# Inverse roots of the norms per head: root function of ScalarE and reciprocal, or Newton steps on VectorE

## The chip, the core and the metric

The kernel runs on one core of a Trainium2 chip. The metric is the device time in microseconds (us) of one execution. The median of 3 runs of the kernel before is 2390.03 us (2385.15 to 2393.97). The engines are TensorE (PE; its weight loads are listed as PEld), VectorE (DVE), ScalarE (ACT), GpSimd (POOL) and SyncE (SP, which issues the DMAs).

## The reference

One step of a two-layer backbone over 384 tokens (128 of context, 256 latent) of width 1024, in fp32. Each layer is a gated FFN, a mixer and a second gated FFN, each with a residual and a layer norm. The mixer projects its input once and feeds three branches: window attention, neighbourhood attention and a recurrence (RWKV-7) of 8 heads of 64 channels in two directions. Two places in the recurrence's branch normalise per head:

```python
kk = split_heads((k * lp['k_k']).astype(f32), C_HEADS)
kk = kk / jnp.maximum(jnp.sqrt(jnp.sum(kk * kk, axis=-1, keepdims=True)), 1e-12)
...
mu = y.mean(-1, keepdims=True)
var = jnp.mean(jnp.square(y - mu), -1, keepdims=True)
yn = ((y - mu) * lax.rsqrt(var + GN_EPS)).reshape(B, L, C_WIDTH) * lp['gn_g'] + lp['gn_b']
```

## The kernel before, in words

Activations lie with the channels on the partitions and the 384 tokens along the free axis. All big products are made from weights and activations split into a high and a low part (three matmuls for each block of 128 x 128). The weights stream in units of 8 blocks: a DMA brings `raw`, ACT copies it to `hi`, DVE subtracts to get `lo` (`fetch`, called by `Stream.take`).

A layer runs FFN 1, the mixer, FFN 2. The mixer has three stages. In `attention` the eight head pairs of the two attentions (`heads_pair`: scores, a softmax on DVE and ACT, transposes and products with the values) run beside `front_fill`, a generator of projections and gates; the first pieces of the recurrence's projections (`conv_gen` with the names tw, al, k0, r0, v0, k1, r1, v1) are among them. In the second stage `rwkv_gen` works through four pairs of heads p = 0 to 3. For each pair, `rwkv_prepare` makes decays and keys, `rwkv_chunks` solves small triangular systems for chunks of 64 tokens (DVE steps that depend on each other, small matmuls, copies out of PSUM), and `rwkv_scan` carries the state over the chunks, normalises the output per head, and multiplies by the gate. The solve of pair p runs beside the scan of pair p-1 and the preparation of pair p+1. Beside all of it `mixer_fill` supplies dense work for PE: the remaining projections (`conv_gen` for gl, k2, r2, v2, k3, r3, v3), the gates of branches B and C (a tanh on ACT each; those of C are stored to DRAM as `gcd`) and the projection of branch B. In the third stage the C gates come back, branch C is projected (`proj_c`, tile `pp`), the branches are added, and the output projection (`w_out`) and the layer norm follow.

What sets the order: the program is traced in Python, the generators yield costs and `add`, `beside` and `step` draw so much dense work for so much work of the recurrence or attention; `tc.issue_after` ties traced instructions behind a given one on their engine, and `tc.high_priority` lifts pieces (weights, preparation, scan, solve) ahead of others by an offset. A scheduler then orders each engine's instructions by these priorities and by what is ready, and inserts the waits. Each engine works through its own list in that order. Loads of ACT's function tables are put into ACT's list where the next function needs another table.

The two places of the change:

- The norm of k, in `conv_gen` (L1304 to L1319): the projection `k0` to `k3` is squared on ACT, and the closure `norms` runs when the next projection has come to its second pair of blocks. `head_sums` makes the sums over each head's 64 channels by three small matmuls into `kss` (tokens on the partitions, 3 token blocks x 2 heads = 6 columns), ACT takes the root, DVE the maximum with 1e-12 and the reciprocal, into `rn0` to `rn3`. The result is used in `rwkv_prepare`: `head_spread` copies it (DVE, tile `rb`) and transposes it back (PE, tile `spread`), and `nkk` is multiplied by it.
- The norm of the recurrence's output, at the end of `rwkv_scan` (from L1738): the centred output is squared on ACT (`gsq`), summed (`gss`), ACT takes the root of the mean plus a constant, DVE the reciprocal (`grn`). `head_spread` follows, then DVE multiplies `k` by it, POOL adds, ACT and POOL split the sum into `och` and `ocl`, the input of `proj_c`.

There are 4 norms of either kind in each layer, 16 in all. The layer norms use the root function too (tiles `warm` and `dd`, 6 norms) and are not touched. All engine calls of DVE, ACT and POOL go through the helper `issue`, so the profile gives them one line, L291; they are told apart by tiles.

Of the kernel before, what the change touches and what calls it, by code (L numbers as in the profile page):

```python
# [8 lines left out]

F32 = mybir.dt.float32  # L10
F32R = mybir.dt.float32r
AF = mybir.ActivationFunctionType
ALU = mybir.AluOpType
AX = mybir.AxisListType

P = 128
# [8 lines left out]
HD = 64  # L25
ALPHA = float((2 * DEPTH) ** 0.25)
LN_EPS = 1e-5
GN_EPS = 64e-5
# [268 lines left out]
def trunk(tc, I, O, order, taps=None, stop=None):  # L297
# [3 lines left out]
    V, S, G, T = Engine(nc.vector), Engine(nc.scalar), Engine(nc.gpsimd), nc.tensor  # L301
# [22 lines left out]
    def C(name, rows=P):  # L324
        o, n = CONST_COLS[name]
        src = conM if name in ("asel", "asel2", "osel") else conA[0] if name in ("rot", "cos", "sin", "maska", "maskb") else con
        return src[:rows, o : o + n]
# [14 lines left out]
    class Stream:  # L342
# [24 lines left out]
        def fetch(self, offset=0):  # L367
# [3 lines left out]
            self.unit += 1  # L371
            hi = ring.tile([P, UNIT * P], F32R, tag="hi", bufs=2, name="hi")
            lo = ring.tile([P, UNIT * P], F32R, tag="lo", bufs=2, name="lo")
            S.activation(out=hi, in_=raw, func=AF.Copy)
# [133 lines left out]

    zs = [tuple(act.tile([P, NTOK + 4], F32R, name=f"{n}{c}") for n in ("zh", "zl")) for c in range(KD)]
    hs = [(zh[:, :NTOK], zl[:, :NTOK]) for zh, zl in zs]  # L510
# [771 lines left out]
    def conv_gen(l, keep, pool, w, names):  # L1282

        wsh = vcol(l, "w_shift")
        late = []
        for nm in names:
            i = C_INDEX[nm]
            pz = mmp("pc")
            for n, cost in enumerate(mm3_steps(pz[:, :NTOK], stream.take("w_in", l, C_ORDER[i], KD), hs)):
                if n == 1 and late:  # L1290
                    late.pop()()
                yield cost
            o = keep.tile([P, NTOK], F32, tag=("r" if nm[0] == "r" else nm), bufs=(2 if nm[0] == "r" else 1), name=nm)
            S.activation(out=o, in_=pz[:, :NTOK], func=AF.Copy, scale=wsh[:, 3 * i + 1 : 3 * i + 2])
            for a, b in STREAMS:
                V.scalar_tensor_tensor(out=o[:, a + 1 : b], in0=pz[:, a : b - 1], scalar=wsh[:, 3 * i : 3 * i + 1], in1=o[:, a + 1 : b], op0=ALU.mult, op1=ALU.add)
                V.scalar_tensor_tensor(out=o[:, a : b - 1], in0=pz[:, a + 1 : b], scalar=wsh[:, 3 * i + 2 : 3 * i + 3], in1=o[:, a : b - 1], op0=ALU.mult, op1=ALU.add)
            w[nm] = o
            if nm == "tw":
                S.activation(out=o, in_=o, func=AF.Tanh)  # L1300
            elif nm == "gl":
                S.activation(out=o, in_=o, func=AF.Tanh, scale=0.5)
                V.tensor_scalar(out=o, in0=o, scalar1=0.5, scalar2=0.5, op0=ALU.mult, op1=ALU.add)
            elif nm[0] == "k":  # L1304

                p = int(nm[1])
                sq = gate_tile(keep)
                S.activation(out=sq, in_=o, func=AF.Square, scale=vcol(l, "k_k")[:, p : p + 1])

                def norms(p=p, sq=sq):  # L1310
                    pss = mmp("kss")
                    head_sums(pss, sq)
                    w[f"rn{p}"] = rn = keep.tile([P, 6], F32, name=f"rn{p}")
                    S.activation(out=rn, in_=pss[:, 0:6], func=AF.Sqrt)
                    V.tensor_scalar(out=rn, in0=rn, scalar1=1e-12, scalar2=None, op0=ALU.max)
                    V.reciprocal(rn, rn)

                late.append(norms)
            elif nm == "al":  # L1319
                ka = keep.tile([P, 2, 4], F32, name="ka2")  # L1320
                V.tensor_scalar(out=ka[:, 0], in0=vcol(l, "k_a"), scalar1=0.5, scalar2=None, op0=ALU.mult)
                V.tensor_scalar(out=ka[:, 1], in0=vcol(l, "k_a"), scalar1=-0.5, scalar2=1.0, op0=ALU.mult, op1=ALU.add)
                w["ka"] = ka
                hb = keep.tile([P, 2, 8], F32, name="hb")
                V.tensor_scalar(out=hb[:, 0], in0=vcol(l, "decay_w0"), scalar1=0.5, scalar2=None, op0=ALU.mult)
                V.tensor_scalar(out=hb[:, 1], in0=vcol(l, "iclr_a0"), scalar1=0.5, scalar2=None, op0=ALU.mult)
                w["hb"] = hb
            yield 0.96
            yield 0.0

    def head_sums(out, sq):

# [350 lines left out]
    def rwkv_scan(l, p, w, pool, keep, oc, x):  # L1683

        mt, nt, yt, rp, pcs = (x[n] for n in ("mt", "nt", "yt", "rp", "pcs"))
# [52 lines left out]
        pst = rwp("gss")  # L1738
        head_sums(pst, sq)
        rn = pool.tile([P, 6], F32, tag="grn", bufs=1, name="grn")  # L1740
        S.activation(out=rn, in_=pst[:, 0:6], func=AF.Sqrt, bias=C("geps"), scale=1.0 / HD)
        V.reciprocal(rn, rn)
        V.tensor_tensor(out=k, in0=k, in1=head_spread(pool, rn), op=ALU.mult)
        G.tensor_tensor(out=k, in0=k, in1=v, op=ALU.add)
        oh = keep.tile([P, NTOK], F32R, tag=f"o{p}h", name=f"och{p}")
# [6 lines left out]
    with es:  # L1752
        with tc.tile_pool(name="init", bufs=1) as pool:
# [15 lines left out]
            for c0 in range(0, KD, 2):  # L1769

                offset = 9000 - 1000 * c0
                i, cols = c0 // 4, slice(256 * (c0 % 4), 256 * (c0 % 4) + 512)
# [10 lines left out]
                for c in range(c0, c0 + 2):  # L1783
                    t = pool.tile([P, NTOK], F32, name=f"xt{c}")
# [51 lines left out]
```

## Time and profile before

| | |
|---|---|
| median of 3 runs | 2390.03 us (2385.15 to 2393.97) |
| profiled execution, its own time | 2388.39 us |
| its span | 2386.7 us |
| mean granted TensorE clock in it | 0.987 of full speed |

In a row of the profile, `out<-in` are tiles by the program's names, the shapes are partitions x elements, `xN` counts instructions. A group ends with the idle time of its engine just before its instructions and what ended most of it; in a timeline that stands in brackets. Times in timelines and stretches count from the span's start. Busy times of PE take in matmuls whose ends are modelled.

### The profile page before, as it was taken

How to read it: one execution, taken by the hardware profiler on the slowest of the kernel's cores; microseconds unless marked ns; L12 is line 12 of the kernel's file. 1: busy time of each engine (PE TensorE's matmuls, PEld its weight loads, DVE VectorE, ACT ScalarE, POOL GpSimd, SP SyncE). 2: the span in 40 equal slices, each digit the busy share in tenths (PEclk: the TensorE clock that was granted, in tenths of full speed). 3: DMA queues.
4: the chain of work that ended last, by engine and by line, in shares of the span. 5: the costliest groups of instructions: out<-in, count | busy, mean ns of one | idle time of the engine just before them, and what ended most of it. 6: DMA issues, size and time to landing. Idle time of an engine off the chain costs nothing.

```text
span 2386.7 us, 42611 instructions
## 1 busy us (share of the span) xinstructions
PE 2279.3 (96%) x17066; PEld 2095.7 (88%) x17066; DVE 1689.0 (71%) x3045; ACT 1074.4 (45%) x1978; POOL 261.6 (11%) x314
## 2 busy tenths in 40 slices
PE   8999999998899999999999999899989999999998
PEld 6999988887777789999989999889877777999997
DVE  3896877767767568876879955776687674775544
ACT  3333345655545445333343333555645454553333
POOL 1000030002122022000020000300023120230000
PEclk9999999999899999999999999999999999999999
DMA  8775643242111262665647733523321112633332
GB/s 310 249 240 183 204 136 105 88 114 69 40 59 48 73 214 98 217 209 174 194 142 234 241 120 129 151 91 102 96 72 42 50 51 75 226 124 133 124 124 89
DMA packets 125077, 324.52 MB, mean 136 GB/s; under 512 B 31568, under 2 KB 50256, under 8 KB 124880
## 3 DMA queue, kind: packets, MB, share of 16 engines
q1 hardware_dynamic: 124880, 321.81, 41.6%
q8 instruction: 134, 2.20, 0.4%
q14 instruction: 63, 0.52, 0.1%
HBM read 312.06 MB, written 9.70 MB: 135 GB/s over the span
## 4 chain that ended last, share of the span: by engine, by line
PE 76%; DVE 11%; ACT 5%; issue 2%; POOL 2%; DMA 1%; SPq 1%; ACTq 0%; POOLq 0%; DVEq 0%
PE po L402 6%; PE po L401 6%; PE po L403 6%; PE pa L385 4%; PE pa L386 4%; PE pg L385 4%; PE pg L386 4%; PE pa L387 4%; PE pg L387 4%; DVE lo L291 3%; PE pz L401 2%; ACT hi L291 2%; PE pz L402 2%; PE pz L403 2%; DVE gt L291 1%
## 5 line engine op out<-in xcount | busy, mean ns | idle before, releaser
L291 ACT ACTIVATE hi<-raw 128x1024 fp32r<-128x1024 f32 x418 | 441.8, 1058 | 728.6 <-issue 236.0
L291 DVE TENSOR_TENSOR lo<-raw,hi 128x1024 fp32r<-128x1024 f32 (+1 forms) x472 | 533.7, 1140 | 273.3 <-ACT hi L291 270.7
L291 DVE SCALAR_TENSOR_TENSOR acc<-adaw,cs,acc 128x1024 f32<-128x1024 f32 x224 | 277.4, 1278 | 0.0
L401 PE MATMUL po<-uh,hi 128*128 128x384 f32 x704 | 237.8, 338 | 0.0
L403 PE MATMUL po<-uh,lo 128*128 128x384 f32 x704 | 236.2, 336 | 0.0
L402 PE MATMUL po<-ul,hi 128*128 128x384 f32 x704 | 236.2, 336 | 0.0
L385 PE MATMUL pa<-zh,hi 128*128 128x384 f32 x584 | 198.7, 340 | 0.0
L386 PE MATMUL pa<-zl,hi 128*128 128x384 f32 x584 | 197.4, 338 | 0.0
L385 PE MATMUL pg<-zh,hi 128*128 128x384 f32 x584 | 197.2, 338 | 0.0
L387 PE MATMUL pa<-zh,lo 128*128 128x384 f32 x584 | 196.4, 336 | 0.6 <-DVE lo L291 0.6
L386 PE MATMUL pg<-zl,hi 128*128 128x384 f32 x584 | 196.6, 337 | 0.0
L387 PE MATMUL pg<-zh,lo 128*128 128x384 f32 x584 | 196.2, 336 | 0.0
L401 PE MATMUL pz<-zh,hi 128*128 128x384 f32 x352 | 127.5, 362 | 8.3 <-ACT hi L291 2.8
L401 PEld LDWEIGHTS po<-uh,hi 128*128 128x128 f32 x704 | 132.3, 188 | 1.4 <-issue 0.8
L402 PEld LDWEIGHTS po<-ul,hi 128*128 128x128 f32 x704 | 132.3, 188 | 0.5
L403 PEld LDWEIGHTS po<-uh,lo 128*128 128x128 f32 x704 | 132.3, 188 | 0.0
L403 PE MATMUL pz<-zh,lo 128*128 128x384 f32 x352 | 125.6, 357 | 1.5 <-DVE lo L291 1.5
L402 PE MATMUL pz<-zl,hi 128*128 128x384 f32 x352 | 124.3, 353 | 0.0
L385 PEld LDWEIGHTS pa<-zh,hi 128*128 128x128 f32 x584 | 109.6, 188 | 4.9 <-ACT hi L291 3.7
L291 POOL TENSOR_TENSOR ax<-ax,hrs 128x384 f32<-128x384 f32 x10 | 9.9, 1015 | 927.1 <-DMA raw<-ws 652.3
L387 PEld LDWEIGHTS pa<-zh,lo 128*128 128x128 f32 x584 | 110.2, 189 | 0.9 <-DVE lo L291 0.9
L387 PEld LDWEIGHTS pg<-zh,lo 128*128 128x128 f32 x584 | 110.1, 189 | 0.0
(395 smaller groups left out, 5219.8 us busy)
## 6 DMA issues: line engine op xcount, KB each, us to landing
raw<-ws SPq DMA_DIRECT2D x418, 512.0 KB, 3.5
adaw<-wada SPq DMA_DIRECT2D x144, 512.0 KB, 4.5
bm<-rpb SPq DMA_DIRECT2D x64, 64.0 KB, 8.0
axd<-ax SPq DMA_DIRECT2D x16, 192.0 KB, 3.7
gcd<-gt SPq DMA_DIRECT2D x16, 192.0 KB, 4.7
gc<-gcd SPq DMA_DIRECT2D x16, 192.0 KB, 3.5
ax<-axd SPq DMA_DIRECT2D x16, 192.0 KB, 4.7
xt<-xt SPq DMA_DIRECT2D x8, 192.0 KB, 8.6
```

Of the source, the lines that this page charges most:

```text
L291: self.last = f(*a, **k)
L385: T.matmul(out, wh, xh, start=first, stop=False)
L386: T.matmul(out, wh, xl, start=False, stop=False)
L387: return T.matmul(out, wl, xh, start=False, stop=last)
L401: T.matmul(out, wh, xh, start=(k == 0), stop=False)
L402: T.matmul(out, wh, xl, start=False, stop=False)
L403: T.matmul(out, wl, xh, start=False, stop=(k == n - 1))
```

## The change

Both roots are taken without ACT. The sum (for k: its maximum with 1e-24, in place of the later maximum of the root with 1e-12; for the output: the mean plus the same constant) goes from PSUM to an SBUF tile on DVE; a first guess of the inverse root is made from the bits of the number, read as an integer; and four Newton steps of three DVE instructions each follow. The tiles `nt6` and `gn6` are new, of 12 columns, one buffer each.

```diff
+I32 = mybir.dt.int32
...
                     w[f"rn{p}"] = rn = keep.tile([P, 6], F32, name=f"rn{p}")
-                    S.activation(out=rn, in_=pss[:, 0:6], func=AF.Sqrt)
-                    V.tensor_scalar(out=rn, in0=rn, scalar1=1e-12, scalar2=None, op0=ALU.max)
-                    V.reciprocal(rn, rn)
+                    nt = keep.tile([P, 2, 6], F32, tag="nt6", bufs=1, name="nt6")
+                    V.tensor_scalar(out=nt[:, 0], in0=pss[:, 0:6], scalar1=1e-24, scalar2=None, op0=ALU.max)
+                    inverse_root(rn, nt)
...
+    def inverse_root(y, nt):
+
+        a, t = nt[:, 0], nt[:, 1]
+        V.tensor_scalar(out=y.bitcast(I32), in0=a.bitcast(I32), scalar1=-0.5, scalar2=1597463007.0, op0=ALU.mult, op1=ALU.add)
+        for i in range(4):
+            V.tensor_tensor(out=t, in0=y, in1=y, op=ALU.mult)
+            V.scalar_tensor_tensor(out=t, in0=t, scalar=-0.5, in1=a, op0=ALU.mult, op1=ALU.mult)
+            V.scalar_tensor_tensor(out=y, in0=t, scalar=1.5, in1=y, op0=ALU.add, op1=ALU.mult)
...
         rn = pool.tile([P, 6], F32, tag="grn", bufs=1, name="grn")
-        S.activation(out=rn, in_=pst[:, 0:6], func=AF.Sqrt, bias=C("geps"), scale=1.0 / HD)
-        V.reciprocal(rn, rn)
+        nt = pool.tile([P, 2, 6], F32, tag="gn6", bufs=1, name="gn6")
+        V.tensor_scalar(out=nt[:, 0], in0=pst[:, 0:6], scalar1=1.0 / HD, scalar2=GN_EPS, op0=ALU.mult, op1=ALU.add)
+        inverse_root(rn, nt)
         V.tensor_tensor(out=k, in0=k, in1=head_spread(pool, rn), op=ALU.mult)
```

## Rows read from the trace of the kernel before

**Rows 1.** The page: busy time by engine, and the chain that ended last

```profile
PE 2279.3 (96%) x17066; PEld 2095.7 (88%) x17066; DVE 1689.0 (71%) x3045; ACT 1074.4 (45%) x1978; POOL 261.6 (11%) x314
...
PE 76%; DVE 11%; ACT 5%; issue 2%; POOL 2%; DMA 1%; SPq 1%; ACTq 0%; POOLq 0%; DVEq 0%
```

**Rows 2.** Busy time by stretch, the two recurrences: us, then busy per engine (instructions)

```profile
563.00:860.00 297.00, 274.74 (x3473) 226.93 (x3474) 204.83 (x429) 147.21 (x273) 63.18 (x91) 0.97 0.20 62
1740.00:2040.00 300.00, 277.36 (x3491) 229.72 (x3490) 208.29 (x434) 148.47 (x275) 66.22 (x91) 0.97 0.20 63
```

**Rows 3.** Groups by line and shape, ACT: busy us, mean ns of one, idle before

```profile
L291 ACT ACT_TABLE_LOAD x40 | 51.3, 1283 | 22.8 <-DMA gcd<-gt 8.9 <-DMA axd<-ax 5.5 <-DVE ax L291 5.3
...
L291 ACT ACTIVATE grn<-gss,con 128x6 f32<-128x6 f32 x8 | 2.1, 267 | 0.1
...
L291 ACT ACTIVATE rn<-kss 128x6 f32<-128x6 f32 x8 | 1.4, 177 | 1.2 <-PE kss L1334 1.1
```

**Rows 4.** Groups by line and shape, DVE

```profile
L291 DVE TENSOR_TENSOR si<-si,pg 128x384 f32<-128x384 f32 x73 | 40.3, 552 | 73.3 <-PE pg L387 73.2
...
L291 DVE SCALAR_TENSOR_TENSOR gt<-gt,pp 128x384 f32<-128x384 f32 x16 | 8.7, 546 | 7.9 <-PE pp L403 7.9
...
L291 DVE RECIPROCAL grn<-grn 128x6 f32<-128x6 f32 x8 | 1.5, 189 | 5.6 <-ACT grn L291 5.6
...
L291 DVE TENSOR_SCALAR rn<-rn 128x6 f32<-128x6 f32 x8 | 1.3, 165 | 3.6 <-ACT rn L291 3.6
```

**Rows 5.** Timeline of DVE, the solve's small dependent steps: start, us, instruction

```profile
784.24 0.17 DVE L291 COPY gt<-l 128x2 f32<-128x2 f32 x1
...
784.84 0.18 DVE L291 TENSOR_TENSOR pr<-l,gt 128x18 f32<-128x18 f32 x1
```

**Rows 6.** Timeline of ACT, the first root of layer 0

```profile
449.19 1.28 ACT L291 ACT_TABLE_LOAD   x1
450.48 0.18 ACT L291 ACTIVATE rn<-kss 128x6 f32<-128x6 f32 x1
```

**Rows 7.** The chain in order of time: the first and last of its whole table loads

```profile
449.19 1.28 ACT L291
...
2030.11 1.28 ACT L291
```

**Rows 8.** Busy time by stretch, behind the first root

```profile
453.00:455.00 2.00, 1.67 (x8) 1.23 (x8) 1.11 (x3) 1.95 (x6) 0.00 (x0) 1.00 0.00 0
```

**Rows 9.** Timeline around the second root of layer 0: idle before, in brackets

```profile
547.18 0.17 DVE L291 TENSOR_SCALAR nm<-nm 128x2 f32<-128x2 f32 x1
...
552.31 0.17 DVE L291 RECIPROCAL sm<-sm 128x2 f32<-128x2 f32 x1 [1.26 <-ACT pe L291]
...
552.71 0.65 PE L1094 MATMUL po<-ptl,vt 128*64 128x256 f32 x2 [1.82 <-ACT ptl L291]
...
554.80 1.54 PE L1094 MATMUL po<-ptl,vt 128*64 128x256 f32 x5 [0.63 <-ACT ptl L291]
```

**Rows 10.** Timeline behind the third root of layer 0, DVE and PE

```profile
616.72 0.55 DVE L291 TENSOR_TENSOR nkk<-nkk,spread 128x384 f32<-128x384 f32 x1 [4.52 <-PE spread L1368]
...
626.74 1.14 PE L1364 MATMUL pm<-gt,atq 64*64 64x128 f32 x24 [0.40 <-ACT uv L291]
```

**Rows 11.** Timeline of DVE behind the third recurrence root of layer 0

```profile
832.21 0.29 DVE L291 TENSOR_TENSOR mt<-pm,con 128x128 f32<-128x128 f32 x1 [4.96 <-PE pm L1364]
```

**Rows 12.** Timeline at the end of layer 0's recurrence

```profile
850.81 0.19 DVE L291 RECIPROCAL grn<-grn 128x6 f32<-128x6 f32 x1 [0.27 <-ACT grn L291]
...
854.02 0.55 DVE L291 TENSOR_TENSOR k<-k,spread 128x384 f32<-128x384 f32 x1
...
854.70 0.44 PE L401 MATMUL pp<-och,hi 128*128 128x384 f32 x1 [0.87 <-ACT gt L291]
...
856.26 0.61 PE L401 MATMUL pp<-och,hi 128*128 128x384 f32 x2 [0.25 <-ACT och L291]
...
857.34 0.44 PE L402 MATMUL pp<-ocl,hi 128*128 128x384 f32 x1 [0.47 <-POOL ocl L291]
```


## The prediction

> **What bounds the kernel now.** I read the page first, for the busy shares and the chain that ended last. TensorE (PE) is busy 96% of the span, 2279.3 of 2386.7 us, and 76% of the chain is its own work; VectorE (DVE) holds 11% of the chain, ScalarE (ACT) 5% [rows 1]. So all that PE could lose or win back over the whole kernel is 107 us, and an engine beside it counts only where PE is seen to wait for it. Next come the two stretches in which the roots of the recurrence and half of those of k stand: PE is busy 274.74 of 297.00 us in layer 0 and 277.36 of 300.00 us in layer 1, so that 22.3 and 22.6 us are open there; DVE is at 69%, ACT at 50% [rows 2]. DVE is the busier of the two engines between which work moves. Then come the groups by line and shape: 40 table loads of 1283 ns, 51.3 us in all, and two kinds of root, eight of each [rows 3]. The rest is the order of time at the single roots, which decides: what stands behind a root on its engine, and what PE waits for.
>
> **What the change removes.** 16 roots go, 8 x 177 and 8 x 267 ns, 3.6 us of ACT [rows 3]. Table loads go with them. In the timeline of ACT a load stands right in front of a root (1.28 us at 449.19, root at 450.48) [rows 6], and another in front of the next exp, tanh or their like. In each layer 7 of the 8 roots have such a pair; the first root of the recurrence follows the last root of k without a switch. That makes 28 of the 40 loads, 28 x 1.283 = 35.9 us of ACT. The other 12 belong to the layer norms' roots and to the first function; they stay. DVE loses 8 maxima and 16 reciprocals, and 9.2 us of waiting for the root (3.6 and 5.6) [rows 4].
>
> **What it adds.** Each root becomes 14 instructions on six columns: one that fits the sum, one that makes the first guess from the bits, and four rounds of three. The trace has no fused multiply of six columns. With an immediate factor the fused form takes 546 ns on 384 columns where the plain product takes 552 [rows 4], so I price it like the plain small ones, at 165 ns [rows 4]. They depend on each other, so what counts is their pitch: the solve's small dependent steps start at 784.24 and, three steps on, at 784.84, which is 0.20 us each [rows 5]. A root then takes 14 x 0.20 = 2.8 us of DVE's queue, 2.4 us more than the two instructions of k's norm, 2.6 more than the one of the recurrence. Over 16 roots that is 8 x 2.4 + 8 x 2.6 = 40.0 us, less the 9.2 us of waiting: 31 us more on DVE, against 39.5 us less on ACT. The guess on integer bits is in no row. It lies between 0.15 us, a little under the nearest row, and twice the 165 ns of that row; I take the row itself, for it is the same instruction and shape [rows 4]. The upper end would add 16 x 0.165 = 2.6 us to DVE. No DMA and no POOL instruction is added or moved.
>
> A rule speaks against the change. The trace shows 0.20 us per dependent small step whatever it computes [rows 5]. The Trainium skill, VectorE: DVE Perf Modes, section Rules for kernel authors, says that chained Vector instructions should not be judged by their work: keep their count low, since each one pays its own flush. The trace agrees; by this rule the 200 more instructions alone decide, and that is the slower rival below.
>
> **Where it meets PE's path.** The chain holds eight whole loads, from 449.19 to 2030.11, 8 x 1.28 = 10.3 us [rows 7]; the other 20 lie beside PE's work, and removing them gains nothing that can be seen here. Four places per layer follow, in layer 0's numbers; layer 1 repeats them.
>
> First root of k (attention): two loads fall out in front of the exps. PE is idle 2.00 - 1.67 = 0.33 us behind them [rows 8]. Ends: 0.33 gained, or 2.4 lost if the steps are put in front of the query's subtraction, for which the scores wait. I take 0.33, since DVE has no longer to wait for ACT there.
>
> Second root (end of attention): the softmax's maximum is out at 547.35, but its reciprocal runs only at 552.31, behind ACT, and PE waits 1.82 and 0.63 us for the transposed weights [rows 9]. Without the loads, 2 x 1.28 us, the exps end so much earlier. Ends: nothing, if the 2.4 us more of DVE stand in front of the reciprocal, and 2.45, if both waits go. I take 1.8: the first wait goes and the second stays, since the softmax is traced ahead of the norm and comes first where both are ready.
>
> Third root (the solve of the first pair): its second load delays the tanh, the exps and the copies behind it, for which PE waits 0.40 us at 626.74. The steps are covered: DVE sits idle 4.52 us soon after [rows 10]. Ends: 0.40 and the whole load of 1.28; I take 0.40, as PE has a backlog there. No loss: cover of 4.52 against 2.4. If that cover were gone, 2.4 would be lost.
>
> Fourth root and the first three of the recurrence: nothing. Behind the third DVE idles 4.96 us for PE [rows 11], longer than 2.6. If the cover is gone, each costs up to 2.6.
>
> Last root (end of the recurrence): here the root is on the path. The old reciprocal starts at 850.81 and ends at 851.00. If the new steps start when it did, they end at 850.81 + 2.8 = 853.6, some 2.5 us later than it did. The next user, the product with the spread root, starts at 854.02 [rows 12], so 3.0 us lie between the reciprocal and it, and the copy and the three transposes that spread the root need a part of these. PE's wait of 0.87 us for a gate's tanh behind a table load goes, but its last wait, for the low half of the output, ends at 857.34 and sets the start of the rest [rows 12]. Ends: 1.28 gained (the load is on the chain, and the gate's store and reload start earlier), 2.5 lost (all of the delay goes through). I take 0.7 lost, near the middle, since part of the 3.0 us swallows it.
>
> **The sum.** Per layer -0.33 - 1.8 - 0.4 + 0.7 = -1.83, for two layers -3.7 us. The profiled execution took 2388.39 us (span 2386.7), 1.6 under the median of 2390.03, and the sum is made against its waits; from it the forecast would be 2384.7. I carry the difference over to the median: **2386.3 us**, no difference that counts (0.5%, about what a measurement of this kernel can tell from no change, is 12 us). The ends give 2 x (-0.33 - 2.45 - 1.28 - 1.28) = -10.7 and 2 x (2.4 + 0 + 0 + 2.5) = +9.8: 2379.3 to 2399.8.
>
> **Rivals.** *The loads weigh more than the waits show.* For it: they stand on the chain at eight places; with ACT freed 39 us earlier, the next weights are split earlier too. Price: the eight loads, 10.3 us, and what PE's waits at the second root have beyond a load, 2 x (2.45 - 1.28) = 2.3: 2390.0 - 12.6 = 2377.4, faster by 0.53%. Against it: PE is busy around most of them. The trace shows the root 0.01 us after the load's end, and no gap in front [rows 6]. The Trainium skill, ScalarE: Activation LUTs, section What ACT_TABLE_LOAD costs, gives about 2.66 us for a switch, half of it a drain. By it, an estimate, the 28 switches would be 74 us of ACT. The rows do not show the second half. Chance of this rival 0.19.
>
> *The Newton steps set the end.* Place: DVE from the solve on, where it is at 69%; mechanism: the 14 steps run in one piece ahead of the copies out of PSUM and of the solve's steps, and PE, whose order is fixed, stands behind them. Price: at the fourth root 2.4, at the second and third of the recurrence 2.6 each, at the last 2.5, together 10.1, less the 0.33 + 1.8 + 0.4 = 2.5 gained elsewhere: 7.6 per layer, 15.2 in all, 2405.2 us, slower by 0.64%. It decides from the point at which DVE's idle time behind a root is under 2.6 us. Against it: the idle stretches of 4.52 and 4.96 us [rows 10, 11]. Chance 0.12.
>
> *The loads stay.* The loads could be needed by other functions, and only the roots go. Against it: they come in pairs around a root. Then DVE's steps stay uncovered at the end alone: 2390.0 + 2 x 2.5 = 2395.0, still within 0.5%. Chance 0.03.
>
> **Chances and range.** The forecast, with all the small sums about it, has 0.66. Within 0.5% also lies the rival of the loads that stay: 0.69 together. Faster by over 0.5% 0.19, slower 0.12. The range takes in the ends of the unknown costs and reaches to the faster rival: 2376 to 2400; what is left out is the slower rival and the tail of the other, less than 2 in 10.
>
> **What would show it.** 12 table loads instead of 40 and ACT's busy time down from 1074.4 by 39 us [rows 1]; DVE's busy time up by 200 instructions of 0.16, about 32 us. Steps at a pitch of 0.20 us: a pitch of 0.3 would make a root 4.2 us and bring the slower rival. Right at the second root if PE's waits for the transposed weights fall from 2.45 us to about 0.6; wrong if the softmax's reciprocal stands behind the steps. Right at the end if PE's last wait there ends 0.7 us later against the last sums; wrong if it moves by over 2 us. The forecast fails as a whole if PE waits for DVE's small steps inside the solve, or if the order of the matmuls changes far from the roots.

## The result, and the profile after

The changed kernel takes **2420.26 us** (2419.44 to 2422.03) where the kernel before, measured beside it, takes 2389.16: ratio 1.0133, interval 1.0118 to 1.0147. It is slower by some 31 us; the forecast was 2386.3 and its range ended at 2400.

The page of the changed kernel, busy time by engine (answers to [rows 1]):

```profile
PE 2307.8 (95%) x17066; PEld 2117.5 (88%) x17066; DVE 1706.5 (71%) x3245; ACT 1036.0 (43%) x1934; POOL 264.6 (11%) x314
```

The same two stretches of the recurrences as in [rows 2]; the third figure from the end is TensorE's granted clock:

```profile
563.00:860.00 297.00, 275.63 (x3415) 225.71 (x3414) 208.48 (x493) 128.73 (x248) 60.76 (x85) 0.93 0.17 53
1740.00:2040.00 300.00, 276.98 (x3373) 225.82 (x3372) 210.97 (x499) 133.73 (x261) 59.98 (x89) 0.93 0.16 51
```

PE carries out the same 17066 matmuls and is busy 28.5 us longer. What it is idle has hardly changed: 2417.7 - 2307.8 = 109.9 us of the span against 107.4, and 21.4 us of the first stretch against 22.3. The reader who looks only for new waits finds nothing of the right size. The granted clock has changed: 0.93 in both stretches against 0.97, 0.975 over the span against 0.987.

The groups of the steps and of the loads by line and shape (answer to [rows 3, 4]):

```profile
L292 ACT ACT_TABLE_LOAD x12 | 15.4, 1283 | 14.5 <-DMA axd<-ax 6.6 <-DVE ax L292 5.3 <-DMA cc<-cc 2.4
L292 DVE SCALAR_TENSOR_TENSOR grn<-gn,grn 128x6 f32<-128x6 f32 x32 | 8.4, 261 | 0.7
...
L292 DVE TENSOR_TENSOR nt<-rn 128x6 f32<-128x6 f32 x32 | 5.1, 161 | 0.3
...
L292 DVE TENSOR_SCALAR rn<-nt 128x6 int32<-128x6 int32 x8 | 1.3, 162 | 0.1
```

The 28 loads are gone, the guess on integer bits costs what the nearest row said (162 ns), and where nothing stands between them the steps follow each other at the pitch of 0.20 us, as DVE's timeline at the end of layer 0 shows:

```profile
854.78 0.17 DVE L292 TENSOR_SCALAR grn<-gn 128x6 int32<-128x6 int32 x1
854.98 0.17 DVE L292 TENSOR_TENSOR gn<-grn 128x6 f32<-128x6 f32 x1
...
857.19 0.17 DVE L292 SCALAR_TENSOR_TENSOR grn<-gn,grn 128x6 f32<-128x6 f32 x1
```

So nearly every operation does what it was priced at (four of the 32 in the second row took 0.88 to 0.995 us, which is why its mean is 261 ns), and the time still comes out elsewhere. Where it is lost is read by laying the starts of the same matmuls in layer 0 side by side:

| first matmul of | before, us | after, us | difference |
|---|---|---|---|
| the first solve's small products (pz from yr) | 606.6 | 602.0 | -4.6 |
| the second solve's pq | 649.6 | 653.3 | +3.7 |
| the third solve's pq | 721.1 | 730.6 | +9.5 |
| the last norm's sums (gss) | 849.2 | 853.7 | +4.5 |
| the output projection (po) | 871.4 | 879.7 | +8.3 |
| the layer norm's root on ACT (dd) | 916.4 | 930.5 | +14.2 |

Attention ends earlier, as forecast and by more than forecast. In the first solve, which holds the third root of k, 8.3 us are lost, and in the second 5.8; the third and fourth win 5.0 back; behind the last norm, in the merge of the branches and up to the layer norm, 9.7 are lost. Layer 1 repeats it: the last of these marks comes 31 us late there.

Two places account for it. The first is the granted clock around the first solve. Stretches of 10 us, before:

```profile
600.00:610.00 10.00, 7.17 (x218) 6.21 (x216) 9.40 (x16) 5.74 (x11) 0.00 (x0) 0.96 0.34 107
610.00:620.00 10.00, 10.00 (x125) 8.38 (x119) 4.84 (x13) 3.87 (x6) 0.00 (x0) 0.53 0.06 9
620.00:630.00 10.00, 8.99 (x125) 6.18 (x117) 3.31 (x8) 8.34 (x18) 1.43 (x4) 0.98 0.14 51
630.00:640.00 10.00, 9.72 (x137) 8.41 (x136) 7.80 (x14) 5.31 (x11) 5.83 (x12) 0.85 0.04 11
640.00:650.00 10.00, 8.45 (x82) 6.27 (x82) 7.43 (x13) 4.30 (x9) 2.63 (x4) 1.00 0.03 8
...
670.00:680.00 10.00, 9.46 (x138) 7.66 (x137) 9.12 (x19) 6.39 (x13) 5.51 (x10) 1.00 0.26 78
680.00:690.00 10.00, 10.00 (x169) 9.64 (x169) 9.10 (x21) 4.91 (x7) 4.56 (x6) 1.00 0.36 109
```

and after:

```profile
600.00:610.00 10.00, 8.00 (x212) 7.01 (x214) 7.24 (x15) 4.94 (x10) 0.00 (x0) 0.63 0.18 57
610.00:620.00 10.00, 10.00 (x122) 7.34 (x123) 4.29 (x20) 3.52 (x7) 0.00 (x0) 0.50 0.17 54
620.00:630.00 10.00, 10.00 (x156) 8.11 (x154) 5.63 (x14) 6.07 (x15) 3.48 (x5) 0.84 0.01 2
630.00:640.00 10.00, 6.32 (x56) 4.36 (x52) 3.71 (x4) 4.26 (x9) 4.12 (x9) 0.67 0.05 14
640.00:650.00 10.00, 9.71 (x54) 7.39 (x54) 6.47 (x11) 1.15 (x3) 4.29 (x5) 0.65 0.01 2
...
670.00:680.00 10.00, 9.04 (x223) 6.13 (x221) 9.08 (x18) 6.37 (x13) 4.84 (x6) 0.72 0.23 75
680.00:690.00 10.00, 10.00 (x94) 8.11 (x88) 4.83 (x11) 3.21 (x5) 5.25 (x10) 0.77 0.07 19
```

The share that is missing from 1.00, times 10 us, is clock time lost: 0.4 + 4.7 + 0.2 + 1.5 = 6.8 us before, 3.7 + 5.0 + 1.6 + 3.3 + 3.5 + 2.8 + 2.3 = 22.2 us after, 15.4 more in 90 us. PE stands at 1.2 GHz in these stretches instead of 2.4; a matmul of 128x384 in them follows the one before by 0.32 us, in stretches at full clock by 0.175. (The Trainium skill, TensorE: Matmul & The Clock Gate, section Terms, puts the penalty of throttled time at that time multiplied by the share of the clock that is not granted; that is the sum just made, and the marks in the table above move by about as much.)

The second place is the merge. DVE's timeline there, before (start, length, instruction, idle before it):

```profile
862.58 1.09 DVE L291 SCALAR_TENSOR_TENSOR gc<-gc,pp 128x384 f32<-128x384 f32 x2
...
865.22 1.37 DVE L291 SCALAR_TENSOR_TENSOR ml<-ax,mh 128x384 fp32r<-128x384 f32 x1
866.76 0.56 DVE L291 SCALAR_TENSOR_TENSOR ml<-ax,mh 128x384 fp32r<-128x384 f32 x1 [0.17 <-ACT mh L291]
867.24 1.01 DVE L291 SCALAR_TENSOR_TENSOR gc<-gc,pp 128x384 f32<-128x384 f32 x2
```

and after:

```profile
863.63 0.55 DVE L292 SCALAR_TENSOR_TENSOR gc<-gc,pp 128x384 f32<-128x384 f32 x1
865.86 0.56 DVE L292 SCALAR_TENSOR_TENSOR ml<-ax,mh 128x384 fp32r<-128x384 f32 x1 [1.69 <-ACT mh L292]
866.34 0.55 DVE L292 SCALAR_TENSOR_TENSOR gc<-gc,pp 128x384 f32<-128x384 f32 x1
...
869.98 0.55 DVE L292 SCALAR_TENSOR_TENSOR gc<-gc,pp 128x384 f32<-128x384 f32 x1
```

The instructions are the same; only their order on DVE differs. Before, two gated products `gc` are made, then the two remainders `ml`: 867.24 - 862.58 = 4.66 us for two tiles. After, each product stands behind the remainder of the tile before it, and that waits 1.69 us for ACT's `mh`, which waits for POOL's sum of the very product just made: 869.98 - 863.63 = 6.35 us for two tiles. Neither instruction is part of the change, and both lie hundreds of us behind the third root.

### The profile page after: what moved, and what is told of

Its sections match the earlier page's. It is cut to its first block, busy times and chain, and to the rows that moved or that the text cites. A ratio compares the mean times of both kernels' runs of the same rounds, so it can differ in the third digit from the quotient of the medians.

```text
span 2417.7 us, 42767 instructions
## 1 busy us (share of the span) xinstructions
PE 2307.8 (95%) x17066; PEld 2117.5 (88%) x17066; DVE 1706.5 (71%) x3245; ACT 1036.0 (43%) x1934; POOL 264.6 (11%) x314
```

## The experiments

Two accounts were set against each other: **the steps** (the 14 small steps on DVE cost where they stand) and **the order** (each engine's list is drawn up before the run, from costs and priorities; with other instructions in it, it comes out in another order far from the roots). The table is the whole study. The product of span and mean granted clock, a mean over the executions, stands for the span at full clock; it is rough, since it treats waits as if they followed the clock too. The last column is counted in the programs' lists: the smallest number of PE's 13862 lines that must be put in elsewhere to turn the list of before into this one (idle matmuls that were added count too; lines with the same tiles and shapes count as the same). A matmul in fp32 can stand in the profile twice, so the profile has 17066 matmuls for these lines.

| kernel | median us | ratio to before, interval | clock | span x clock | PE lines |
|---|---|---|---|---|---|
| before (77 executions beside these) | 2389.3 | | 0.987 | 2356 | 0 |
| the change | 2420.3 | 1.0133 (1.0118 to 1.0147) | 0.975 | 2358 | 696 |
| e1 no root, no steps | 2426.6 | 1.0153 (1.0135 to 1.0170) | 0.967 | 2346 | 822 |
| e2 root and steps | 2420.7 | 1.0127 (1.0110 to 1.0144) | 0.981 | 2372 | 430 |
| e3 norms of k only | 2442.3 | 1.0211 (1.0195 to 1.0228) | 0.965 | 2354 | 838 |
| e4 output norms only | 2391.5 | 1.0003 (0.9993 to 1.0012) | 0.986 | 2357 | 54 |
| f1 third root only | 2437.7 | 1.0205 (1.0174 to 1.0235) | 0.967 | 2357 | 832 |
| f2 all but the third | 2401.3 | 1.0052 (1.0032 to 1.0072) | 0.982 | 2359 | 452 |
| f3 sums in pairs | 2404.8 | 1.0067 (1.0044 to 1.0090) | 0.977 | 2348 | 696 |
| f4 scaling on GpSimd | 2430.5 | 1.0166 (1.0138 to 1.0195) | 0.970 | 2355 | 884 |
| g1 changed, wait filled | 2417.5 | 1.0134 (1.0113 to 1.0154) | 0.978 | 2363 | 726 |
| g2 before, wait filled | 2404.2 | 1.0077 (1.0058 to 1.0095) | 0.984 | 2365 | 322 |
| g3 pairs, wait filled | 2410.0 | 1.0100 (1.0076 to 1.0124) | 0.976 | 2350 | 726 |
| g4 part, pairs | 2385.5 | 0.9984 (0.9968 to 1.0001) | 0.985 | 2349 | 68 |
| h1 changed, 24 mixed in | 2450.9 | 1.0264 (1.0245 to 1.0283) | 0.970 | 2375 | 670 |
| h2 changed, 12 mixed in | 2427.7 | 1.0175 (1.0153 to 1.0196) | 0.976 | 2368 | 726 |
| h3 before, 12 mixed in | 2415.1 | 1.0108 (1.0087 to 1.0129) | 0.982 | 2369 | 322 |
| h4 as g4, again | 2386.5 | 0.9992 (0.9977 to 1.0007) | 0.985 | 2348 | 68 |
| i1 first two roots of k | 2385.1 | 0.9986 (0.9973 to 0.9999) | 0.985 | 2349 | 14 |
| i2 outputs, pairs | 2386.6 | 0.9992 (0.9975 to 1.0008) | 0.988 | 2356 | 54 |

### Root or steps

e1 leaves the norms per head out: in place of root and steps one DVE instruction writes a constant. e2 keeps ACT's root and DVE's reciprocal and runs the four Newton rounds on top.

```diff
...
-inverse_root(rn, nt)
+V.tensor_scalar(out=rn, in0=pss[:, 0:6], scalar1=0.0, scalar2=0.125, op0=ALU.mult, op1=ALU.add)
...
```

```diff
+S.activation(out=rn, in_=nt[:, 0], func=AF.Sqrt)
 inverse_root(rn, nt)
...
-V.tensor_scalar(out=y.bitcast(I32), in0=a.bitcast(I32), scalar1=-0.5, scalar2=1597463007.0, op0=ALU.mult, op1=ALU.add)
+V.reciprocal(y, y)
...
```

> Each of the 16 roots becomes one DVE instruction that writes a constant, 0.125, in place of the inverse root; the normalisation per head is left out, and with it both the roots on ACT and the Newton steps. Theory of the steps (the 200 more DVE instructions hold PE up): with no steps and no loads it must be no slower than the kernel before, 2375 to 2392 us. Theory of the order (each engine's list of instructions comes out differently once the roots are off ACT, and PE loses its time to the new lists): the lists show the same two marks as the changed kernel (the scaling of r ahead of the copies of y on ACT, and on DVE no two sums of branch C next to each other), so it is as slow as the changed kernel, 2408 to 2422 us.

> ACT takes the root as before and DVE its reciprocal, and the four Newton steps run on top of it on DVE: all the loads and all the steps. Theory of the steps: as slow as the changed kernel or slower, 2418 to 2430 us. Theory of the order: the lists lie between the two kernels (6 of 8 pairs of sums of branch C are left, one scaling of r stands ahead of one copy of y), so 2392 to 2410 us.

e1 is slower than the change itself and above both of its ranges, with neither a root nor a step of these norms in it, so the steps are not what the loss needs. It does not show that they are free: its lists differ from those of the change too (596 lines of PE), and its product of span and clock is 12 us lower. e2 fits the number of the steps but not for their reason alone: its product is 15 us above before (root, steps and 44 loads are all paid), the rest is clock. The order's size was missed there.

### Which norms

e3 is the change with the output norm put back, e4 the change with the norm of k put back.

```diff
...
-inverse_root(rn, nt)
+S.activation(out=rn, in_=pst[:, 0:6], func=AF.Sqrt, bias=C("geps"), scale=1.0 / HD)
+V.reciprocal(rn, rn)
```

```diff
...
-inverse_root(rn, nt)
+S.activation(out=rn, in_=pss[:, 0:6], func=AF.Sqrt)
+V.tensor_scalar(out=rn, in0=rn, scalar1=1e-12, scalar2=None, op0=ALU.max)
+V.reciprocal(rn, rn)
```

> Newton steps for the norms of k alone; the norms of the output keep the root. Theory of the steps: about half of the 31 us, 2400 to 2408 us. Theory of the order: its lists bear both marks of the changed kernel, so most of the loss is here, 2408 to 2422 us.

> Newton steps for the norms of the output alone; the norms of k keep the root. Theory of the steps: about half of the 31 us, 2400 to 2408 us, most of it at the end of the recurrence, where the root is on the path. Theory of the order: r and y stand as in the kernel before and half of the pairs of sums are left, so 2391 to 2402 us.

The loss sits in the norms of k. With the output norms alone nothing changes: there are 28 loads in e4 in place of 40, and its product is that of before, so that neither the small steps in the recurrence nor the 12 loads show in the time. e3 is worse than the change, by more than either account said.

### Which root of k

```diff
+if p in (2,):
...
     inverse_root(rn, nt)
+else:
+    S.activation(out=rn, in_=pss[:, 0:6], func=AF.Sqrt)
+    V.tensor_scalar(out=rn, in0=rn, scalar1=1e-12, scalar2=None, op0=ALU.max)
+    V.reciprocal(rn, rn)
```

This is f1, where p counts the roots of k from 0. f2 has (0, 1, 3) there, i1 has (0, 1). f1 and i1 keep the root function for the output norms; f2 has Newton steps for them. (There are eight output norms, four per layer; the expectation of f1 says six.)

> Only the third root of k in each layer (the one taken while the solve of the first pair runs) goes by Newton steps; the other three roots of k and all six roots of the output norms stay as they were (36 loads of a function table instead of 40). Order theory: this one root turns the order of the engines' lists (the scaling of r ahead of the split of the first pair's y on ScalarE, the branch sums of the merge one by one instead of in pairs), so it is slow as the whole change is: 2410 to 2440 us. Rival, each root of k costs where its steps stand: the whole loss spread over four roots, a quarter of it here, 2395 to 2403 us. A second rival, the second root is the one that counts (its steps are on the path in attention's end): 2388 to 2392 us.

> The whole change except the third root of k, which keeps the root function (16 loads). Order theory: the lists of the solve and of the recurrence's start keep the order of before, half of the branch sums stay in pairs as in the run with the output norms alone (2391.5 us), and the end of attention gains what it gained in the changed kernel, 4.6 us per layer: 2380 to 2386 us, faster than the kernel before by 0.15 to 0.4 percent. Rival, each root of k costs where its steps stand: three quarters of the loss, 2410 us or more.

> Only the first two roots of k in each layer go by Newton steps; the third and fourth root of k and the output norms stay with the root function (32 loads), and the lists of the recurrence and of the merge keep the order of before. If the terms of the prediction for these two roots hold (0.33 and 1.8 us per layer): 2383 to 2387 us. If the end of attention gains the 4.6 us per layer that it gained in the changed kernel and nothing is given back: 2377 to 2383 us. If the earlier start of the first solve meets a longer stretch at half clock, as in the changed kernel: 2386 to 2394 us.

One root out of eight per layer, the third of k, brings more than the whole loss. Replacing it moves 832 of PE's lines, 138 of ACT's 1884 and 288 of DVE's 3047 (24 of these are the new steps). f2 is a miss for both accounts: without the third root most of the loss goes, not all; the fourth root, replaced alone, moves 426 of PE's lines (this list was drawn up, not run), and f2 has 452. i1 is the cleanest test of the forecast's own terms: with the first two roots alone, 14 lines of PE move, and the time is 4.1 us below that of before, where the terms for these two roots give 2 x (0.33 + 1.8) = 4.3. The interval allows any gain from 0.2 to 6.5 us, so that the closeness is in part luck. Its PE waits at the second root, where before had 1.82 and 0.63 us [rows 9]:

```profile
547.79 0.92 PE L1015 MATMUL pt<-con,pe 128*128 128x128 f32 x6 [0.42 <-DVE nt L292]
549.29 0.86 PE L1095 MATMUL po<-ptl,vt 128*64 128x256 f32 x5 [0.58 <-ACT ptl L292]
```

### The merge and the scaling of r

f3 is the change with this edit in the merge (`then(V)` ties what follows behind the last instruction traced for DVE, so that both products of a pair come first; the DMAs that fetch `ax` again are issued in pairs as well):

```diff
-    S.activation(out=mh, in_=ax[m], func=AF.Copy, scale=0.5)
-    V.scalar_tensor_tensor(out=ml, in0=ax[m], scalar=0.5, in1=mh.bitcast(F32), op0=ALU.mult, op1=ALU.subtract)
...
+    for i in (m - 1, m) if m % 2 else ():
...
+        S.activation(out=mh, in_=ax[i], func=AF.Copy, scale=0.5)
+        with then(V):
+            V.scalar_tensor_tensor(out=ml, in0=ax[i], scalar=0.5, in1=mh.bitcast(F32), op0=ALU.mult, op1=ALU.subtract)
...
+        nc.sync.dma_start(out=ax[i], in_=spill[:, i])
```

f4 is the change with this one at the end of `rwkv_prepare`:

```diff
-S.activation(out=r, in_=r, func=AF.Copy, scale=vcol(l, "r_k")[:, p : p + 1])
+G.tensor_scalar(out=r, in0=r, scalar1=vcol(l, "r_k")[:, p : p + 1], scalar2=None, op0=ALU.mult)
```

> The changed kernel, with the sums of the last branch in the merge put back in pairs on VectorE (both sums of a pair of tiles, then both remainders), as the kernel before has them. In the changed kernel this stage took 6.35 us for two tiles against 4.6 us, and TensorE waited for it at the output projection. Order theory with this place as a term: 6.7 us per layer come back, 2404 to 2412 us. Rival, TensorE is as late at the start of the output projection for other reasons and the sums only fill the wait: 2418 to 2422 us.

> The changed kernel, with the scaling of r moved from ScalarE to GpSimd, so that no such copy stands ahead of the split of the first pair's y on ScalarE. Order theory with this place as a term: the wait of 3.7 us in front of the block that needs the split goes, 7 us in all, 2410 to 2415 us; if the lower granted clock of the stretch behind it (0.50 to 0.84 from 600 to 650 us, and 0.72 and 0.77 from 670 to 690 us) comes from that wait too, up to 14 us per layer come back, 2385 to 2400 us. Rival, the wait only covers another one: 2418 to 2422 us.

f3 moves four instructions per layer on DVE's list, none on PE's, ACT's or POOL's, and three DMA issues per layer on SP's, and gains 2420.3 - 2404.8 = 15.5 us: half of the loss is the order in the merge. Which of the four instructions and the three issues count was not taken apart. The largest group of PE's waits between 855 and 945 us in the changed kernel (us in total, times, longest):

```profile
PE po L402 <- ACT mh L292: 3.4, 2, 2.4
```

and between 860 and 945 us in f3:

```profile
PE po L403 <- DVE ml L292: 1.1, 2, 0.9
```

The longest of these waits in the changed kernel comes with low clock as well. PE's timeline, and the 10 us behind it:

```profile
888.51 0.44 PE L402 MATMUL po<-mh,hi 128*128 128x384 f32 x1 [2.41 <-ACT mh L292]
890.00:900.00 10.00, 10.00 (x51) 10.00 (x51) 5.32 (x16) 4.56 (x11) 0.00 (x0) 0.86 0.78 264
```

The kernel before and f3 have no wait of PE over 1.2 us in the merge, and in f3 the clock is 1.00 from 880 to 900 us.

f4 misses all of its ranges. It took away the wait that it was meant to take, 3.7 us of PE for `yt` (the split of the first pair's y on ACT) behind the scaling of r, and got two others in its place; the lists moved again (884 lines). The wait that goes, from the changed kernel's list of PE's waits in layer 0's mixer:

```profile
PE pb L1378 <- ACT yt L292: 4.8, 2, 3.7
```

and what f4 has instead:

```profile
PE pm L1374 <- ACT atq L292: 3.1, 1, 3.1
PE pb L1378 <- DVE bk L292: 2.4, 2, 2.1
```

So an edit that only moves one instruction of each pair to another engine, and takes a wait away, made this kernel slower by 10 us. What that wait itself costs stays open.

### The clock

In all kernels the product of span and clock stays between 2346 and 2375 us, and in the change it is 2358 against 2356: read so, its whole loss is clock, 2358 / 0.975 against 2358 / 0.987 being 29 us. (Gains and losses cancel in that product: with the merge's order mended, in f3, it is 2348, and with the steps left out, in e1, 2346.) That time follows the clock at one and the same list can be read from repeats: f2's seven executions run from 2397.2 us (clock 0.984) to 2418.4 us (0.975), the executions of the kernel before have a median of 2395.1 us at 0.984 (7 of them) and of 2383.8 at 0.989 and above (16). What was tried next was to keep PE's clock up by filling its wait of 2.42 us at the start of the first solve, or by mixing dense work between the small products behind it.

g1 (the change), g2 (before) and g3 (f3) have this ahead of the first step of small products of the first solve (48 matmuls in the program, x96 in the profile):

```diff
...
+fl = atp("fl")
+with tc.issue_after(bon_last[p].ins), tc.high_priority(offset=600):
+    for _ in range(12):
+        T.matmul(fl[:, :NTOK], hs[0][0][:, 0:P], hs[0][0], start=True, stop=True)
```

h1 (the change) has one such matmul behind every 4 of its small products in the traced order, h2 (the change) and h3 (before) behind every 8:

```diff
...
+with tc.issue_after(rw_last[0].ins), tc.high_priority(offset=1500):
+    T.matmul(fl[:, :NTOK], hs[0][0][:, 0:P], hs[0][0], start=True, stop=True)
```

> The changed kernel, with 12 more matmuls of 128x384 per layer, whose result nobody reads, put into the one wait of 2.42 us of TensorE at the start of the first solve (between the sum for the bonus and the first 96 small products); all other work and its order stay. They take 12 x 0.175 = 2.1 us at full clock, less than the wait. Clock theory: the span times the mean granted clock is the same 2357 us in the kernel before (0.987) and in the changed one (0.975), so the loss of 31 us is low clock, and the wait is what sets the clock to a half behind it (602.7 to 623 us, 20 us, in the changed kernel): with the wait filled the clock stays up there, some 10 us per layer come back, 2398 to 2412 us, and the mean granted clock is 0.979 to 0.984. Rival, the clock falls for the 192 small products behind the wait or for something else: 2418 to 2426 us.

> The kernel before with the same 12 matmuls in the same wait. In it the clock is at a half for only some 10 us behind this wait (609.6 to 619.3 us). Clock theory: up to 5 us per layer come back, 2379 to 2386 us. Rival, the small products set the clock: 2388 to 2394 us.

> The changed kernel with both: the sums of the last branch in pairs (2404.8 us alone) and the filled wait. Clock theory: the two add up, 2385 to 2396 us. Rival: 2403 to 2410 us.

> The changed kernel, with one idle matmul of 128x384 (its result is not read) behind every 4 of the small products in the first two steps of the first solve: 24 per layer, 24 x 0.175 = 4.2 us at full clock. All roots go by Newton steps as before (12 loads). The extra matmuls turn the lists back to the order of the kernel before: the split of the first pair's y ahead of the scaling of the second r on ScalarE, and half of the branch sums in pairs. Order theory: what the order costs comes back but the extra matmuls are paid, 2392 to 2402 us. Clock theory, in which the small products without dense work between them lower the clock: the half clock from 602 to 624 us goes as well, 2382 to 2394 us. If neither holds: 2424 to 2432 us.

> The same with 12 idle matmuls per layer (behind every 8 small products), 2.1 us per layer at full clock. The lists stay in the order of the changed kernel. Order theory: no gain, 2420 to 2428 us. Clock theory: the half clock behind the small products is shorter or gone, up to 10 us per layer less 2, 2404 to 2416 us.

> The kernel before with the same 12 idle matmuls per layer, its lists in the order they had. Order theory: the matmuls are paid, 2389 to 2396 us. Clock theory: the half clock from 609.6 to 619.3 us goes, up to 5 us per layer less 2: 2382 to 2388 us.

(The mixing stands in the first two steps of that solve, 48 matmuls each, x96 in the profile.) All six miss what the clock theory expected of them. In g1 the wait is filled and the next opens one step on, as PE's timeline shows:

```profile
598.21 2.54 PE L1614 MATMUL fl<-zh 128*128 128x384 f32 x12
601.16 0.98 PE L1375 MATMUL pz<-yr,gt 16*32 16x16 f32 x96 [0.40 <-DVE yr L292]
604.40 0.83 PE L1344 MATMUL kss<-con,gt 128*128 128x2 f32 x6 [2.25 <-ACT gt L292]
```

and in h3 the low clock is longer than in the kernel before, not shorter (stretches of 10 us):

```profile
600.00:610.00 10.00, 7.55 (x99) 5.79 (x97) 9.31 (x16) 5.22 (x9) 0.00 (x0) 0.92 0.32 107
610.00:620.00 10.00, 10.00 (x138) 6.82 (x138) 0.41 (x3) 1.79 (x3) 0.00 (x0) 0.50 0.01 2
620.00:630.00 10.00, 10.00 (x115) 7.92 (x116) 4.60 (x11) 4.07 (x7) 0.00 (x0) 0.50 0.17 54
630.00:640.00 10.00, 9.75 (x96) 7.30 (x96) 1.47 (x2) 6.45 (x16) 0.31 (x2) 0.72 0.00 0
```

The expectations of g2 and h3 rested on a false premise too: these 12 matmuls do not leave the lists of the kernel before as they were, 322 lines of PE (24 of them the idle matmuls) and 48 of ACT come out elsewhere. Here too other lists come with lost time, with all roots on ACT and no Newton step at all: 15 and 26 us, of which the idle matmuls' own time is 2 x 2.1 = 4.2 at full clock and 2 x 12 x 0.32 = 7.7 at half. In g1 and h2 the lists stay nearly those of the change (30 lines of PE, 24 of them the idle matmuls of both layers), and the time stays near it: -2.7 and +7.4 us, where the same idle matmuls are paid. h1 was to turn the lists back, judged by two marks in them; counted whole, 670 lines of PE differ from before, and it is the slowest of all.

### Looking for a faster version

g4 and h4, one kernel, take the change as i1 does for k, keep the Newton steps for the outputs, and have f3's merge; i2 is e4 with f3's merge.

```diff
+if p in (0, 1):
...
     inverse_root(rn, nt)
...
+    for i in (m - 1, m) if m % 2 else ():
...
```

> A part of the change that leaves the solve's lists as before: the first two norms of k and all norms of the output by Newton steps, the third and fourth norm of k by the root function, the sums of the last branch in pairs. Order theory alone: 2378 to 2388 us, faster than before by what the end of attention gains (2 to 4.6 us per layer). Clock theory: the span times the granted clock comes to 2345 to 2355 us, but the granted clock follows from where the waits fall and may be anything from 0.975 to 0.988: 2380 to 2412 us.

> The same kernel as the part of the change with the sums in pairs (first two norms of k and all output norms by Newton steps, the third and fourth norm of k by the root function), in more rounds: 2382 to 2388 us, faster than before by 0.1 to 0.3 percent, if what it gained (2385.5 against 2389.0 us) was not chance.

> The norms of the output by Newton steps, those of k by the root function, and the sums of the merge in pairs. The output norms alone took 2391.5 us with the span times the clock as before (2356.5 us). If the pairs give back what four unpaired sums per layer cost there: 2379 to 2386 us. If they were hidden: 2388 to 2394 us.

g4, h4 and i2 cannot be told from the kernel before: each interval holds 1; i2 lies between its two ranges. i1's interval ends just below 1 (0.9999), with 0.14% faster in the middle; among eighteen comparisons one such can be chance. Nothing is faster by 0.5%. Attention ends 7.0 us earlier in i1's layer 0 (first `up` at 554.4 against 561.4 us). Of these, 2.2 are there already at 373 us, ahead of the first root at 449, in a stretch in which the profiled execution of before has low clock. The kernel before, then i1:

```profile
360.00:375.00 15.00, 11.26 (x54) 10.60 (x55) 11.23 (x33) 9.44 (x25) 0.05 (x1) 0.89 0.50 133
360.00:375.00 15.00, 11.88 (x65) 10.61 (x66) 11.41 (x32) 10.59 (x28) 0.00 (x0) 1.00 0.54 148
```

The layer norm's root behind the merge comes 5.0 us earlier in layer 0, and still 5.0 earlier in layer 1: what the second layer gains at the end of its attention, 2.7 us, is lost again. The low clock of the first solve in layer 0 takes twice as long as before:

```profile
600.00:610.00 10.00, 10.00 (x236) 8.85 (x225) 4.16 (x11) 4.61 (x9) 0.00 (x0) 0.50 0.12 45
610.00:620.00 10.00, 10.00 (x91) 7.59 (x91) 4.39 (x9) 4.25 (x7) 0.31 (x2) 0.50 0.16 54
```

## Why the prediction was wrong

**What held.** 28 loads go and ACT's busy time falls by 38.4 us (forecast 39). 200 instructions come, at 0.20 us where nothing stands between them. The waits of the first root go. At the second root PE's waits fall from 2.45 to 0.42 + 0.58 = 1.0 us and attention ends 4.6 us earlier (forecast 2.1 for the first two roots; of the difference 1.7 is the low clock of before at 554 to 558 us, gone). The output norms are neutral (e4). i1 as a whole comes out near the terms of the first two roots (4.1 against 4.3 us), within an interval of 0.2 to 6.5.

**What was mis-sized without harm.** DVE's busy time rises by 17.5 us, not 32. e1 shows why in part: with 8 instructions fewer than before DVE is busy 12.9 us less, so in that order its other instructions run shorter. The last root was to cost 0.7; it costs nothing that PE sees, because 15 matmuls of dense work (`pz`) now stand between the spread of the root and the first `pp` (858.1 to 860.8 us): it has a cover that the trace of before did not have.

**The step that failed** is the third root: "Ends: 0.40 and the whole load of 1.28; I take 0.40, as PE has a backlog there. No loss: cover of 4.52 against 2.4." What it weighed, a wait of 0.40 us and steps of 2.4, is small against what came: this root alone comes with 48 us (f1), and the loss is there without any step (e1). The step took every other instruction to stay where the trace of before has it. The kernel's lists are made anew for every program, and with this root off ACT they come out otherwise for the rest of the layer. The end of the prediction named this ("if the order of the matmuls changes far from the roots") as what would make it fail as a whole; it gave that neither a price nor a chance, and none of its rivals held it. The rival of the Newton steps had the right sign and the wrong mechanism: its place was DVE's queue ahead of the copies, for 10.1 us per layer, and PE's waits for DVE between 600 and 850 us only rose from 10.5 to 12.9 us. The 14 steps do not run in one piece there either: those of the third root stand between 607.2 and 615.7 us, with other DVE instructions among them.

**The two rules** that were weighed did not decide. By the Trainium skill, VectorE: DVE Perf Modes, section Rules for kernel authors, the number of instructions decides; the trace agrees on the 0.20 us each, but e1, without them, is no faster. By the Trainium skill, ScalarE: Activation LUTs, section What ACT_TABLE_LOAD costs, each switch would have given back more than the load; ACT's busy time fell by the loads and roots alone (28 x 1.283 + 3.6 = 39.5 us against 38.4), and the trace shows no drain beyond: the first root starts 0.01 us behind the end of its load [rows 6].

**What is shown and what stays open.** Shown: a loss of this size comes with neither root nor steps (e1); the third root's replacement alone brings it (f1); the order in the merge is 15.5 us of it (f3). Read from the records, not forced by an experiment: the rest is time at the lower granted clock in the solves. Not settled: what the steps cost where the lists move (the products of e1 and e2 leave room for 12 to 15 us at full clock, though both have other lists as well), which of the moved lines lowers the clock, and why it stays low for 10 us in one kernel and 20 in another. An experiment that holds all lists fixed while only the third root changes was not tried; it would need the whole order written out by hand.

## What to carry to other kernels

Where a scheduler draws up the engines' lists, first compare the lists of the two programs; price the change from the trace of before only as far as they agree. Here up to 70 moved lines of PE meant within 0.2% of before, 322 and more meant 0.5 to 2.6% slower, whatever the edit was meant to do, idle work included. The count tells these two groups apart and ranks nothing within the second: h1 has 670 lines and 2.6%, f3 696 and 0.7%. And where the time grows with no new wait, read the granted clock by stretch before looking for a cause in the instructions; a place in which the order matters, as in this merge, is better tied by hand.

## What the runs showed of the hardware

The granted clock fell to one half behind a wait of PE and stayed there while PE's records show it fully busy. Where the first solve starts, the kernel before, the change and i1 have the same wait of 2.4 us for `yr`, followed by the same small products:

```profile
606.59 0.98 PE L1364 MATMUL pz<-yr,gt 16*32 16x16 f32 x96 [2.42 <-DVE yr L291]
602.00 1.10 PE L1374 MATMUL pz<-yr,gt 16*32 16x16 f32 x96 [2.42 <-DVE yr L292]
599.61 1.24 PE L1379 MATMUL pz<-yr,gt 16*32 16x16 f32 x96 [2.43 <-DVE yr L292]
```

The clock is at one half from 609.1, 602.7 and 600.0 us on, for about 10, 20 and 20 us. In the changed kernel it is 0.50 from 610 to 620 us at 10.00 of 10.00 us busy, with 122 instructions, among them small products of 32 rows. Dense matmuls of 128x384 between the small products did not shorten that; in h3 it grew to about 27 us.
